# An attention-times-value kernel: v loaded for eight heads at a time, out stored for eight heads at a time

## Chip, cores, metric

One core of a Trainium2 chip. Times are device microseconds of one execution. Before the change: median 1056.14 us of 3 runs (1055.9 to 1057.2).

## The reference

```python
batch, n_heads, seq, head_dim = 8, 12, 1024, 64
# attn_weights: (8, 12, 1024, 1024) float32 = 403 MB;  v and out: (8, 12, 1024, 64) float32 = 25 MB each
out = np.einsum('bhqs,bhsd->bhqd', attn_weights, v)
```

## The kernel before

96 heads are worked as 24 groups of four (`q`), each group as two units (`n`). 128 partitions hold four heads x 32. A unit is one load of attn of 8.4 MB, cast to bf16 on its way into one of two buffers `abf`. TensorE transposes it (line 124), DVE and ACT copy the transposes out of PSUM, TensorE multiplies with v (line 166), transposes the product back (line 151), and ACT copies the rows into a slot of `osb`. In the first unit of a group v is spread over partitions by TensorE (line 139). GpSimd issues nearly all DMAs; SyncE counts their landings and passes them on. The parts that matter here:

```python
def pe_unit(i, n, loaded, it):                      # TensorE
    pe.wait_ge(*loaded)
    for g in range(G):
        ...
        transpose_g(abf[i], g, n)
    if i == 0:
        pe.wait_ge(s_vr, it)
        spread_v(range(VH), po + px)
        wait_both(s_vbf, it * 2)
    transpose_back()
    ...                                             # multiply
with nc.Fori(1, NV + 1, 1, engines=(PE,)) as it:    # 24 turns, two units each
    ...

def load_v(iv):                                     # GpSimd, 1 MB read
    pool.dma_start(out=vr.rearrange("p b x -> p (b x)"), in_=v_g[iv]).then_inc(s_v, 16)

def store(q, by_sync=False):                        # 1 MB written
    eng = nc.sync if by_sync else pool
    eng.wait_ge(s_out, 2 * q + 3)
    eng.dma_start(out=out_q[q], in_=osb[slot(q)].rearrange("p r d -> p (r d)"),
                  **({} if by_sync else {"single_packet": True}),
    ).then_inc(s_end if by_sync else s_osb[slot(q)], 16)

for n in range(NU - 2):
    pool.wait_ge(s_t[True], (n + 1) * PER_DVE)      # unit n is transposed, its buffer is free
    load_attn(n + 2)
    if n % 2 == 0:
        q = n // 2
        for s in s_sp:
            pool.wait_ge(s, 2 * q + 2)              # v of group q has been spread
        if q + 1 < NV:
            load_v(q + 1)
        if 0 < q <= HELD_FROM:                      # HELD_FROM = 17
            store(q - 1)
for q in range(HELD_FROM, BY_SYNC):                 # held until after the last load: 17, 18, 19
    store(q)
# SyncE: 20, 21, 22 and the pieces of 23, after the last load has landed
```

Of the kernel before, what the change touches and what calls it, by code (L numbers as in the profile page):

```python
# [10 lines left out]
def kernel(  # L11
# [18 lines left out]
    nc = tc.nc  # L30
    fp32 = mybir.dt.float32
    bf16 = mybir.dt.bfloat16
# [3 lines left out]
    D = v.shape[-1]  # L36
    NH = B * H
    P = 128
    VH = 4
    VP = P // VH  # L40
    G = Q // VP // 2
# [3 lines left out]
    SB = S // P  # L45
    VB = S // VP // SB
    NV = NH // VH
    NU = 2 * NV


    HELD = 6
    HELD_FROM = NV - 1 - HELD
    BY_SYNC = HELD_FROM + 3

    BY_EIGHTS = HELD_FROM // 2
    NO = 2 + NV - 2 * BY_EIGHTS

    HALVED = NU - 2

    def slot(q):  # L60
        return q % 2 if q < 2 * BY_EIGHTS else q - 2 * BY_EIGHTS + 2

    attn_q = attn_weights.rearrange("b (hq four) (p r) s -> (b hq) (four p) (r s)", four=VH, p=VP)
    out_q = out.rearrange("b (hq four) (p r) d -> (b hq) (four p) (r d)", four=VH, p=VP)
    v_g = v.rearrange("b (hq four) (p r) d -> (b hq) (four p) (r d)", four=VH, p=VP)

    def on_dve(g):
        return g % 8 in (0, 2, 4, 5, 7)
# [1 line left out]
    def count_of(g):  # L70

        return sum(on_dve(x) == on_dve(g) for x in range(g + 1))
# [4 lines left out]
    with tc.tile_critical(no_gpsimd_drain=True):  # L77
        sem = tc.alloc_semaphore
        sb = lambda name, shape, dt: nc.alloc_sbuf_tensor(name, shape, dt).ap()
# [1 line left out]
        spread = sb("spread", [P, VB, P], bf16)  # L81
        abf = [sb(f"abf{i}", [P, G, S], bf16) for i in range(2)]
        at = sb("at", [P, G, KW, P, 2], bf16)
        v32 = sb("v32", [P, VB, SB * D], fp32)
        vr = sb("vr", [P, VB, SB * D], bf16)
        vbf = sb("vbf", [P, SB, VH, D], bf16)
        ot = sb("ot", [P, GH, P], fp32)
        osb = [sb(f"osb{i}", [P, 2 * G, D], fp32) for i in range(NO)]
        bank = [nc.alloc_psum_tensor(f"bank{i}", [P, 512], fp32).ap() for i in range(8)]
        pt = [b.rearrange("p (k j) -> p k j", k=KW) for b in bank[:4]]  # L90
        po = bank[4:6]
        px = bank[6:8]
# [2 lines left out]
        s_abf = [sem(f"s_abf{i}") for i in range(2)]  # L95
        s_second = {n: sem(f"s_second{n}") for n in range(HALVED, NU)}
        s_v0, s_v = sem("s_v0"), sem("s_v")
        s_osb = [sem(f"s_osb{i}") for i in range(NO)]
        s_end = sem("s_end")

        s_t = {True: sem("s_t_dve"), False: sem("s_t_act")}
        s_sp = [sem("s_sp_dve"), sem("s_sp_act")]
# [8 lines left out]
        s_out, s_fin = sem("s_out"), [sem("s_fin0"), sem("s_fin1")]  # L111
        s_memset, s_const, s_vr = sem("s_memset"), sem("s_const"), sem("s_vr")
# [4 lines left out]
        pe = nc.tensor  # L117
# [13 lines left out]
                )  # L131
            last.then_inc(s_t[on_dve(g)])

        def spread_v(heads, banks):

            for h, ps in zip(heads, banks):
                rows = ds(h * VP, VP)
                for b in range(VB):
                    last = pe.matmul(  # L139
                        out=ps,  # L140
                        lhsT=spread[rows, b],
                        rhs=vr[rows, b],
                        start=(b == 0),
                        stop=(b == VB - 1),
                    )
                last.then_inc(s_sp[h % 2])
# [29 lines left out]
        def wait_both(s, n):  # L176
            for x in s:
                pe.wait_ge(x, n)

        def pe_unit(i, n, loaded, it):  # L180

            pe.wait_ge(*loaded)
            for g in range(G):
                if g == GH:
                    pe.wait_ge(s_half, n)
                transpose_g(abf[i], g, n)
            wait_both(s_ot, n)
            if i == 0:
                pe.wait_ge(s_vr, it)
                spread_v(range(VH), po + px)  # L190
                wait_both(s_vbf, it * 2)
            transpose_back()
            wait_both(s_last, n)
            for hp in range(2):
                for h in range(2):
                    for half in range(2):
                        outs = po[hp][ds(half * D, D), ds(h * GH * VP, GH * VP)]
                        last = multiply(outs, 2 * hp + h, half)
                last.then_inc(s_m[hp])
# [12 lines left out]
        def engine(dve):  # L212
            eng = nc.vector if dve else nc.scalar
# [4 lines left out]
            def spread_copy(h, ps, count):  # L218
                eng.wait_ge(s_sp[e], count)
                copy(  # L220
                    out=vbf[:, :, h], in_=ps.rearrange("p (k d) -> p k d", k=SB)
                ).then_inc(s_vbf[e])
# [7 lines left out]
                )  # L230

            def rows_of(n):
                return osb[slot(n // 2)][:, ds(n % 2 * G, G)]

            def back_copies(rows, count, free=None):
                if free is not None:
# [26 lines left out]
            def unit(n, base, rows, free):  # L263

                of_t, of_sp, of_back, of_m = base
                for g in mine:
                    copy_g(g, of_t + (n * per + count_of(g)))
                if n % 2 == 0:
                    spread_copy(e, po[e], of_sp + (n + 1))
                    spread_copy(2 + e, px[e], of_sp + (n + 2))  # L270
                if not dve:
                    back_copies(rows, of_back + 2 * n, free)
                product(of_m + (n + 1))


            un, iters = (2, NV) if dve else (4, BY_EIGHTS)
            with nc.Fori(1, iters + 1, 1, engines=(DVE if dve else ACT,)) as it:
                base = [eng.snap(it * (un * k) - un * k) for k in (per, 1, 2, 1)]
                of_free = None if dve else eng.snap(it * 2 - 2)
                for n in range(un):  # L280
                    rows = osb[(n - 1) // 2 % 2][:, ds((n - 1) % 2 * G, G)]
                    unit(n, base, rows, of_free + (n + 1) // 2 if n % 2 == 1 and not dve else None)
            for n in range(un * iters, NU):
                unit(n, (0, 0, 0, 0), rows_of(n - 1), None)
            k = 1 - e
            back_copy(rows_of(NU - 1), 4 * k, 4, px[k], 2 * NU + k + 1).then_inc(s_fin[k])

# [3 lines left out]
        for h in range(2):  # L291
            nc.vector.memset(ot[:, :, ds(h * HP, HP)], 0.0).then_inc(s_ot[h])
        nc.vector.wait_ge(s_v0, 16)
        nc.vector.tensor_copy(out=vr, in_=v32).then_inc(s_vr)  # L294
        engine(True)
        engine(False)


        pool = nc.gpsimd
# [8 lines left out]

        def load_v(iv):
            pool.dma_start(  # L310
                out=vr.rearrange("p b x -> p (b x)"), in_=v_g[iv]
            ).then_inc(s_v, 16)

        def store(q, by_sync=False):
            eng = nc.sync if by_sync else pool
            eng.wait_ge(s_out, 2 * q + 3)
            eng.dma_start(  # L317
                out=out_q[q],
                in_=osb[slot(q)].rearrange("p r d -> p (r d)"),
                **({} if by_sync else {"single_packet": True}),  # L320
            ).then_inc(s_end if by_sync else s_osb[slot(q)], 16)

        load_attn(0)
        load_attn(1)
# [2 lines left out]
            out=ident,  # L327
            in_=ident,
            compare_op=mybir.AluOpType.not_equal,
            fill=1.0,  # L330
            base=0,
# [4 lines left out]
        for h in range(VH):  # L336
            pool.wait_ge(s_const, h + 1)
            pool.affine_select(  # L338
                out=spread[ds(h * VP, VP)],
                in_=spread[ds(h * VP, VP)],  # L340
                compare_op=mybir.AluOpType.not_equal,
                fill=1.0,
                base=0,
                pattern=[[1, VB], [-1, P]],
                channel_multiplier=VB,
            ).then_inc(s_const)
        for n in range(NU - 2):
            pool.wait_ge(s_t[True], (n + 1) * PER_DVE)
            load_attn(n + 2)
            if n % 2 == 0:  # L350
                q = n // 2
                for s in s_sp:
                    pool.wait_ge(s, 2 * q + 2)
                if q + 1 < NV:
                    load_v(q + 1)
                if 0 < q <= HELD_FROM:
                    store(q - 1)
        for q in range(HELD_FROM, BY_SYNC):
            store(q)
        pool.drain()  # L360


        nc.sync.dma_start(out=v32.rearrange("p b x -> p (b x)"), in_=v_g[0]).then_inc(s_v0, 16)
        nc.sync.sem_inc(s_free, 2)
        for n in range(-2, NU - 2):

            if n + 2 < HALVED:
                nc.sync.wait_ge(s_abf[n % 2], 16 * ((n + 2) // 2 + 1))
            else:
                nc.sync.wait_ge(s_second[n + 2], 16)  # L370
            nc.sync.sem_inc(s_half)  # L371
            if n >= 0 and n % 2 == 0:
                q = n // 2
                nc.sync.wait_ge(s_v, 16 * (q + 1))
                nc.sync.sem_inc(s_vr)
                if 0 < q <= 2 * (BY_EIGHTS - 1):
                    nc.sync.wait_ge(s_osb[slot(q - 1)], 16 * ((q - 1) // 2 + 1))
                    nc.sync.sem_inc(s_free)
        for q in range(BY_SYNC, NV - 1):
            store(q, by_sync=True)  # L380
        rows = osb[slot(NV - 1)].rearrange("p (u half j) d -> p u half j d", u=2, half=2)
        outs = out_q[NV - 1].rearrange("p (u half j d) -> p u half j d", u=2, half=2, j=GH)
        nc.sync.wait_ge(s_out, NU)
        nc.sync.dma_start(out=outs[:, 0], in_=rows[:, 0]).then_inc(s_end, 16)
        for k in range(2):
            nc.sync.wait_ge(s_fin[k], 1)
            js = ds(4 * k, 4)
            nc.sync.dma_start(out=outs[:, 1, :, js], in_=rows[:, 1, :, js]).then_inc(s_end, 16)
        for q in range(2 * BY_EIGHTS - 2, BY_SYNC):
            nc.sync.wait_ge(s_osb[slot(q)], 16 * BY_EIGHTS if q < 2 * BY_EIGHTS else 16)  # L390
        nc.sync.wait_ge(s_end, 16 * (NV - 1 - BY_SYNC + 3))


# [28 lines left out]
```

## Time and profile before

| | before |
|---|---|
| DMA engines | full in every slice; GpSimd's queue 99.4% of the span |
| bytes at HBM | 453 MB, 430 GB/s |
| TensorE / DVE / ACT busy | 72% / 37% / 38% |
| DMAs | 50 loads of attn, 24 of v, 20 + 6 stores |

The first row bounds the kernel; the others have room. The prediction below shows the lines. From the DMA issues (tile, queue, count, KB at the destination, median us from issue to landing):

```profile
out_dram<-osb POOLq DMA_DIRECT2D x20, 1024.0 KB, 34.2
vr<-in_v_dram POOLq DMA_DIRECT2D x23, 512.0 KB, 34.3
```

The long time to landing is waiting in a full queue.

### The profile page before, as it was taken

What the parts mean: (1) busy time and instruction counts of PE and PEld (TensorE: products, weight loads), DVE (VectorE), ACT (ScalarE), POOL (GpSimd) and SP (SyncE); (2) the same over time, 40 slices, a digit from 0 to 9 for tenths busy, and PEclk for the clock granted to TensorE, in tenths of its full rate; (3) what the DMA queues carried; (4) which work ended last, traced back from release to release, by engine and by line L of the source; (5) the groups of instructions that cost most, each with busy time, mean ns of one, the idle gap of its engine ahead of it and who ended that gap; (6) DMA issues with size and microseconds to landing.
All of it is one profiled execution on the core that took longest, in us unless ns stands there. A gap on an engine that the chain in (4) does not pass through costs nothing.

```text
span 1053.3 us, 16277 instructions
## 1 busy us (share of the span) xinstructions
PE 754.8 (72%) x6920; PEld 709.4 (67%) x6920; DVE 387.9 (37%) x582; ACT 403.3 (38%) x489; POOL 52.4 (5%) x102
## 2 busy tenths in 40 slices
PE   0877686766867578775687766876678768777795
PEld 0776576766867568675686666866667668776785
DVE  1443343333443234432343333433335234433452
ACT  0443344433543334442353333433334334433452
POOL 1000000000000000000000000000000000000000
PEclk9989888888888888898888888888789898898898
DMA  9999999999999999999999999999999999999998
GB/s 219 220 217 208 234 236 218 238 209 247 233 218 238 207 243 239 217 238 209 244 236 215 234 219 237 238 219 234 227 228 234 215 218 218 218 218 215 210 217 322
DMA packets 14662, 239.67 MB, mean 228 GB/s; under 512 B 1600, under 2 KB 2112, under 8 KB 5184
## 3 DMA queue, kind: packets, MB, share of 16 engines
q0 software_dynamic: 13392, 234.36, 99.4%
q1 hardware_dynamic: 1264, 5.24, 1.3%
q8 instruction: 2, 0.03, 0.0%
q14 instruction: 4, 0.03, 0.0%
HBM read 427.82 MB, written 25.17 MB: 430 GB/s over the span
## 4 chain that ended last, share of the span: by engine, by line
DMA 76%; PE 23%; issue 1%; POOL 0%; DVE 0%; ACT 0%; SPq 0%; POOLq 0%
DMA abf<-in_attn_weights_dram 76%; PE bank L124 22%; PE bank L166 0%; PE bank L151 0%; POOL abf L304 0%; DVE osb L227 0%; ACT ot L256 0%; POOLq L417 0%; SPq L371 0%; SPq L77 0%
## 5 line engine op out<-in xcount | busy, mean ns | idle before, releaser
L124 PE MATMUL bank<-ident,abf 128*128 128x128 f32 x3072 | 470.8, 327 | 260.0 <-DMA abf<-in_attn_weights_dram 254.2
L124 PEld LDWEIGHTS bank<-ident,abf 128*128 128x128 f32 x3072 | 461.5, 215 | 272.8 <-DMA abf<-in_attn_weights_dram 266.7
L244 DVE COPY at<-bank 128x1024 bf16<-128x1024 bf16 x480 | 320.3, 689 | 495.1 <-PE bank L124 492.5
L244 ACT COPY at<-bank 128x1024 bf16<-128x1024 bf16 x288 | 289.2, 1012 | 428.1 <-PE bank L124 428.1
L166 PE MATMUL bank<-at,vbf 128*64 128x256 bf16 x3072 | 215.0, 278 | 0.0
L166 PEld LDWEIGHTS bank<-at,vbf 128*64 128x64 bf16 x3072 | 196.7, 108 | 13.4 <-DVE at L244 4.0
L256 ACT COPY ot<-bank 128x512 f32<-128x512 f32 x48 | 28.1, 586 | 181.1 <-PE bank L166 181.1
L256 DVE COPY ot<-bank 128x512 f32<-128x512 f32 x48 | 33.2, 692 | 151.4 <-PE bank L166 151.4
L151 PE MATMUL bank<-ident,ot 128*128 128x128 f32 x392 | 52.2, 276 | 33.0 <-DVE vbf L220 32.2
L151 PEld LDWEIGHTS bank<-ident,ot 128*128 128x128 f32 x392 | 43.4, 141 | 45.0 <-DVE vbf L220 44.0
L304 POOL DMA_DIRECT2D abf<-in_attn_weights_dram x50 | 26.6, 532 | 896.4 <-PE bank L124 895.3
L227 ACT COPY osb<-bank 128x512 f32<-128x512 f32 x97 | 52.2, 589 | 22.5 <-PE bank L151 22.5
L220 DVE CAST vbf<-bank 128x512 bf16<-128x512 f32 x48 | 30.9, 686 | 6.6 <-PE bank L139 6.6
L220 ACT CAST vbf<-bank 128x512 bf16<-128x512 f32 x48 | 25.8, 589 | 11.8 <-PE bank L139 11.8
L139 PE MATMUL bank<-vr,spread 32*128 32x512 bf16 x384 | 25.7, 377 | 0.0
L139 PEld LDWEIGHTS bank<-vr,spread 32*128 32x128 bf16 x384 | 9.9, 92 | 6.9
L310 POOL DMA_DIRECT2D vr<-in_v_dram x23 | 12.1, 528 | 19.2 <-PE bank L139 18.8
L317 POOL DMA_DIRECT2D out_dram<-osb x20 | 10.7, 537 | 37.3 <-ACT osb L227 37.3
L244 ACT ACT_TABLE_LOAD x8 | 10.3, 1283 | 1.2 <-SPq L77 1.1
L294 DVE CAST vr<-v 128x2048 bf16<-128x2048 f32 x1 | 1.4, 1406 | 3.3 <-DMA v<-in_v_dram 3.3
L338 POOL TENSOR_SCALAR_AFFINE_SELECT spread<-spread 32x512 bf16<-32x512 bf16 x4 | 2.5, 629 | 0.6
L227 DVE COPY osb<-bank 128x512 f32<-128x512 f32 x1 | 0.7, 692 | 3.1 <-PE bank L151 3.1
(8 smaller groups left out, 2.1 us busy)
## 6 DMA issues: line engine op xcount, KB each, us to landing
abf<-in_attn_weights_dram POOLq DMA_DIRECT2D x46, 4096.0 KB, 33.2
out_dram<-osb POOLq DMA_DIRECT2D x20, 1024.0 KB, 34.2
vr<-in_v_dram POOLq DMA_DIRECT2D x23, 512.0 KB, 34.3
abf<-in_attn_weights_dram POOLq DMA_DIRECT2D x4, 2048.0 KB, 26.0
out_dram<-osb SPq DMA_DIRECT2D x3, 1024.0 KB, 11.8
v<-in_v_dram SPq DMA_DIRECT2D x1, 1024.0 KB, 4.9
out_dram<-osb SPq DMA_DIRECT2D x1, 512.0 KB, 7.8
out_dram<-osb SPq DMA_DIRECT2D x2, 256.0 KB, 3.0
```

The source lines that it names most:

```text
L124: last = pe.matmul(out=pt[g % 4][:, k], lhsT=words[:, k], rhs=ident, is_transpose=True, start=(k == 0), stop=(k == KW - 1),)
L139: last = pe.matmul(out=ps, lhsT=spread[rows, b], rhs=vr[rows, b], start=(b == 0), stop=(b == VB - 1),)
L151: last = pe.matmul(out=ps[:, ds(j * P, P)], lhsT=ot[:, j0 + j], rhs=ident, is_transpose=True, start=(j == 0), stop=(j == jn - 1),)
L166: last = pe.matmul(out=outs, lhsT=vbf[:, 2 * kw + par, h], rhs=at[:, ds(half * GH, GH), kw, ds(h * VP, VP), par], start=(n == 0), stop=(n ...
L220: copy(out=vbf[:, :, h], in_=ps.rearrange("p (k d) -> p k d", k=SB)).then_inc(s_vbf[e])
L227: return copy(out=rows.rearrange("p (half j) d -> p j half d", half=2)[:, ds(j0, jn)], in_=ps[:, ds(0, jn * P)].rearrange("p (j half d) -> ...
L244: ins = copy(out=at[:, g].rearrange("c k j two -> c (k j two)"), in_=bank[g % 4].bitcast(bf16),)
L256: copy(out=ot.rearrange("c j (h p) -> c h j p", h=VH)[:, ds(2 * e, 2)], in_=po[e].rearrange("c (h j p) -> c h j p", h=2, j=GH),).then_inc( ...
L304: pool.dma_start(out=abf[n % 2][:, ds(g0, gn)].rearrange("p g s -> p (g s)"), in_=attn_q[n // 2][:, ds((n % 2 * G + g0) * S, gn * S)],).th ...
L310: pool.dma_start(out=vr.rearrange("p b x -> p (b x)"), in_=v_g[iv]).then_inc(s_v, 16)
L317: eng.dma_start(out=out_q[q], in_=osb[slot(q)].rearrange("p r d -> p (r d)"), **({} if by_sync else {"single_packet": True}),).then_inc(s_ ...
L338: pool.affine_select(out=spread[ds(h * VP, VP)], in_=spread[ds(h * VP, VP)], compare_op=mybir.AluOpType.not_equal, fill=1.0, base=0, patte ...
```

## The change

The intent: fewer and larger DMAs for v and out. One DMA of v brings eight heads, so TensorE has to pick the half of `vr` by a branch; one store takes eight heads, so ACT's loop runs over sixteen heads (four slots of `osb`) to know its slots. Core of the diff (index helpers, the matching waits of SyncE and the shared buffer for the first v are cut):

```diff
-    HELD_FROM = NV - 1 - HELD          # 17
-    BY_SYNC = HELD_FROM + 3            # 20
+    HELD_FROM = NV - 8                 # 16
+    BY_SYNC = NV - 4                   # 20
...
-        vr = sb("vr", [P, VB, SB * D], bf16)
+        vr = sb("vr", [P, 2, VB, SB * D], bf16)
-        osb = [sb(f"osb{i}", [P, 2 * G, D], fp32) for i in range(NO)]
+        osb = sb("osb", [P, NO, 2 * G, D], fp32)
...
-                spread_v(range(VH), po + px)
+                odd = pe.snap((it - 1) % 2)
+                with pe.If(odd > 0):
+                    spread_v(1, po + px)
+                with pe.Else():
+                    spread_v(0, po + px)
...
-            un, iters = (2, NV) if dve else (4, BY_EIGHTS)
+            un, iters = (2, NV) if dve else (8, LOOPED // 4)
...
-                out=vr.rearrange("p b x -> p (b x)"), in_=v_g[iv]
+                out=vr.rearrange("p two b x -> p two (b x)"), in_=v_2[iv]
...
         for n in range(NU - 2):
+            q, i = n // 2, n % 2
+            if i == 0 and q % 2 == 1 and q + 1 < NV:
+                for s in s_sp:
+                    pool.wait_ge(s, 2 * q + 2)
+                load_v((q + 1) // 2)
             pool.wait_ge(s_t[True], (n + 1) * PER_DVE)
             load_attn(n + 2)
-            if n % 2 == 0:
-                q = n // 2
-                for s in s_sp:
-                    pool.wait_ge(s, 2 * q + 2)
-                if q + 1 < NV:
-                    load_v(q + 1)
-                if 0 < q <= HELD_FROM:
-                    store(q - 1)
+            if i == 0 and q % 2 == 0 and 0 < q <= HELD_FROM:
+                store_2(q - 2)
...
-        nc.sync.dma_start(out=v32.rearrange("p b x -> p (b x)"), in_=v_g[0]).then_inc(s_v0, 16)
+        nc.sync.dma_start(
+            out=v32.rearrange("p (two x) -> p two x", two=2), in_=v_2[0]
+        ).then_inc(s_v0, 16)
```

More of the change, by code (lines that the diff above doesn't have):

```diff
@@ L48 @@
     NU = 2 * NV
-    HELD = 6
-    HELD_FROM = NV - 1 - HELD
-    BY_SYNC = HELD_FROM + 3
-    BY_EIGHTS = HELD_FROM // 2
-    NO = 2 + NV - 2 * BY_EIGHTS
+    HELD_FROM = NV - 8
+    BY_SYNC = NV - 4
+    LOOPED = HELD_FROM
+    NO = 8 + 2
     HALVED = NU - 2
     def slot(q):
-        return q % 2 if q < 2 * BY_EIGHTS else q - 2 * BY_EIGHTS + 2
+        return q % 4 if q < LOOPED + 2 else q - LOOPED + 2
     attn_q = attn_weights.rearrange("b (hq four) (p r) s -> (b hq) (four p) (r s)", four=VH, p=VP)
     out_q = out.rearrange("b (hq four) (p r) d -> (b hq) (four p) (r d)", four=VH, p=VP)
-    v_g = v.rearrange("b (hq four) (p r) d -> (b hq) (four p) (r d)", four=VH, p=VP)
+    out_2 = out.rearrange("b h q d -> (b h) q d").rearrange(
+        "(hq two four) (p r) d -> hq (four p) two (r d)", two=2, four=VH, p=VP
+    )
+    v_2 = v.rearrange("b h q d -> (b h) q d").rearrange(
+        "(hq two four) (p r) d -> hq (four p) two (r d)", two=2, four=VH, p=VP
+    )
     def on_dve(g):
@@ L83 @@
         at = sb("at", [P, G, KW, P, 2], bf16)
-        v32 = sb("v32", [P, VB, SB * D], fp32)
-        vr = sb("vr", [P, VB, SB * D], bf16)
+        vr = sb("vr", [P, 2, VB, SB * D], bf16)
         vbf = sb("vbf", [P, SB, VH, D], bf16)
         ot = sb("ot", [P, GH, P], fp32)
-        osb = [sb(f"osb{i}", [P, 2 * G, D], fp32) for i in range(NO)]
+        osb = sb("osb", [P, NO, 2 * G, D], fp32)
+        v32 = osb[:, ds(NO - 2, 2)].rearrange("p n r d -> p (n r d)")
         bank = [nc.alloc_psum_tensor(f"bank{i}", [P, 512], fp32).ap() for i in range(8)]
@@ L97 @@
         s_v0, s_v = sem("s_v0"), sem("s_v")
-        s_osb = [sem(f"s_osb{i}") for i in range(NO)]
-        s_end = sem("s_end")
+        s_osb = [sem(f"s_osb{i}") for i in range(2)]
+        s_held, s_end = sem("s_held"), sem("s_end")
         s_t = {True: sem("s_t_dve"), False: sem("s_t_act")}
@@ L132, in transpose_g, with spread_v @@
             last.then_inc(s_t[on_dve(g)])
-        def spread_v(heads, banks):
-            for h, ps in zip(heads, banks):
+        def spread_v(two, banks):
+            for h, ps in enumerate(banks):
                 rows = ds(h * VP, VP)
@@ L141, in spread_v @@
                         lhsT=spread[rows, b],
-                        rhs=vr[rows, b],
+                        rhs=vr[rows, two, b],
                         start=(b == 0),
@@ L232, in rows_of @@
             def rows_of(n):
-                return osb[slot(n // 2)][:, ds(n % 2 * G, G)]
+                return osb[:, slot(n // 2), ds(n % 2 * G, G)]
             def back_copies(rows, count, free=None):
@@ L273, in unit @@
                 product(of_m + (n + 1))
-            un, iters = (2, NV) if dve else (4, BY_EIGHTS)
+            un, iters = (2, NV) if dve else (8, LOOPED // 4)
             with nc.Fori(1, iters + 1, 1, engines=(DVE if dve else ACT,)) as it:
                 base = [eng.snap(it * (un * k) - un * k) for k in (per, 1, 2, 1)]
-                of_free = None if dve else eng.snap(it * 2 - 2)
+                of_free = None if dve else eng.snap(it * 2 - 1)
                 for n in range(un):
-                    rows = osb[(n - 1) // 2 % 2][:, ds((n - 1) % 2 * G, G)]
-                    unit(n, base, rows, of_free + (n + 1) // 2 if n % 2 == 1 and not dve else None)
+                    rows = osb[:, (n - 1) // 2 % 4, ds((n - 1) % 2 * G, G)]
+                    free = of_free + n // 4 if n in (1, 5) and not dve else None
+                    unit(n, base, rows, free)
             for n in range(un * iters, NU):
-                unit(n, (0, 0, 0, 0), rows_of(n - 1), None)
+                free = LOOPED // 2 + 1 if n == un * iters + 1 else None
+                unit(n, (0, 0, 0, 0), rows_of(n - 1), free)
             k = 1 - e
@@ L293 @@
         nc.vector.wait_ge(s_v0, 16)
-        nc.vector.tensor_copy(out=vr, in_=v32).then_inc(s_vr)
+        nc.vector.tensor_copy(out=vr.rearrange("p two b x -> p (two b x)"), in_=v32).then_inc(s_vr, 2)
         engine(True)
@@ L310, in load_v, with store, store_2 @@
             pool.dma_start(
-                out=vr.rearrange("p b x -> p (b x)"), in_=v_g[iv]
+                out=vr.rearrange("p two b x -> p two (b x)"), in_=v_2[iv]
             ).then_inc(s_v, 16)
-        def store(q, by_sync=False):
-            eng = nc.sync if by_sync else pool
-            eng.wait_ge(s_out, 2 * q + 3)
+        def store(q, fours, eng, done):
+            eng.wait_ge(s_out, 2 * (q + fours) + 1)
+            at_slot = osb[:, ds(slot(q), fours)].rearrange("p n r d -> p n (r d)")
             eng.dma_start(
-                out=out_q[q],
-                in_=osb[slot(q)].rearrange("p r d -> p (r d)"),
-                **({} if by_sync else {"single_packet": True}),
-            ).then_inc(s_end if by_sync else s_osb[slot(q)], 16)
+                out=out_2[q // 2] if fours == 2 else out_q[q],
+                in_=at_slot if fours == 2 else at_slot[:, 0],
+                **({"single_packet": True} if eng is pool else {}),
+            ).then_inc(done, 16)
+        def store_2(q):
+            store(q, 2, pool, s_osb[q // 2 % 2] if q < HELD_FROM else s_held)
         load_attn(0)
@@ L347 @@
         for n in range(NU - 2):
+            q, i = n // 2, n % 2
[3 more added lines that the diff above has]
+                load_v((q + 1) // 2)
             pool.wait_ge(s_t[True], (n + 1) * PER_DVE)
             load_attn(n + 2)
-            if n % 2 == 0:
-                q = n // 2
-                for s in s_sp:
-                    pool.wait_ge(s, 2 * q + 2)
-                if q + 1 < NV:
-                    load_v(q + 1)
-                if 0 < q <= HELD_FROM:
-                    store(q - 1)
-        for q in range(HELD_FROM, BY_SYNC):
-            store(q)
+            if i == 0 and q % 2 == 0 and 0 < q <= HELD_FROM:
+                store_2(q - 2)
+        for q in range(HELD_FROM, BY_SYNC, 2):
+            store_2(q)
         pool.drain()
-        nc.sync.dma_start(out=v32.rearrange("p b x -> p (b x)"), in_=v_g[0]).then_inc(s_v0, 16)
+        nc.sync.dma_start(
+            out=v32.rearrange("p (two x) -> p two x", two=2), in_=v_2[0]
+        ).then_inc(s_v0, 16)
         nc.sync.sem_inc(s_free, 2)
@@ L373 @@
                 q = n // 2
-                nc.sync.wait_ge(s_v, 16 * (q + 1))
-                nc.sync.sem_inc(s_vr)
-                if 0 < q <= 2 * (BY_EIGHTS - 1):
-                    nc.sync.wait_ge(s_osb[slot(q - 1)], 16 * ((q - 1) // 2 + 1))
+                if q % 2 == 1 and q + 1 < NV:
+                    nc.sync.wait_ge(s_v, 16 * ((q + 1) // 2))
+                    nc.sync.sem_inc(s_vr, 2)
+                if q % 2 == 1 and 1 < q <= HELD_FROM:
+                    nc.sync.wait_ge(s_osb[(q - 3) // 2 % 2], 16 * ((q - 3) // 4 + 1))
                     nc.sync.sem_inc(s_free)
-        for q in range(BY_SYNC, NV - 1):
-            store(q, by_sync=True)
-        rows = osb[slot(NV - 1)].rearrange("p (u half j) d -> p u half j d", u=2, half=2)
+        store(NV - 4, 2, nc.sync, s_end)
+        store(NV - 2, 1, nc.sync, s_end)
+        rows = osb[:, slot(NV - 1)].rearrange("p (u half j) d -> p u half j d", u=2, half=2)
         outs = out_q[NV - 1].rearrange("p (u half j d) -> p u half j d", u=2, half=2, j=GH)
@@ L388 @@
             nc.sync.dma_start(out=outs[:, 1, :, js], in_=rows[:, 1, :, js]).then_inc(s_end, 16)
-        for q in range(2 * BY_EIGHTS - 2, BY_SYNC):
-            nc.sync.wait_ge(s_osb[slot(q)], 16 * BY_EIGHTS if q < 2 * BY_EIGHTS else 16)
-        nc.sync.wait_ge(s_end, 16 * (NV - 1 - BY_SYNC + 3))
+        for k in range(2):
+            nc.sync.wait_ge(s_osb[k], 16 * (HELD_FROM // 4))
+        nc.sync.wait_ge(s_held, 16 * (BY_SYNC - HELD_FROM) // 2)
+        nc.sync.wait_ge(s_end, 16 * 5)
 _INS = ['attn_weights', 'v']
```

## The prediction

> **What bounds the kernel now.** I read the page first (engine shares, slices, queues), then the chain that ended last in order of time, then the busy time by stretch, then the DMA issues and the end of the run.
>
> ```profile
> PE 754.8 (72%) x6920; PEld 709.4 (67%) x6920; DVE 387.9 (37%) x582; ACT 403.3 (38%) x489; POOL 52.4 (5%) x102
> DMA  9999999999999999999999999999999999999998
> q0 software_dynamic: 13392, 234.36, 99.4%
> HBM read 427.82 MB, written 25.17 MB: 430 GB/s over the span
> ```
>
> No compute engine is full, and the 16 DMA engines are full in every slice: the queue fed by GpSimd alone keeps them busy for 99.4% of the span. The GB/s row of the page shows only some 220 because the loads of attn and v are cast on the way and counted at their bf16 size; the bytes at HBM, 427.82 + 25.17 = 453 MB, are what moves, at 430 GB/s.
>
> The chain of waits names TensorE's transposes for 22%, but I do not take that as a bound. In order of time it reads:
>
> ```profile
> 480.20 9.18 PE bank L124 x64
> 489.38 0.28 issue
> 489.67 34.04 DMA abf<-in_attn_weights_dram
> 523.71 0.04 issue
> 523.75 9.54 PE bank L124 x64
> 533.29 0.28 issue
> 533.58 33.69 DMA abf<-in_attn_weights_dram
> ```
>
> The load issued at 533.58 lands 33.7 us later, but a load needs only about 19.3 us of transfer (below). The rest is standing in the queue behind an earlier load. So the transposes decide when a load is issued, not when it starts. The busy time in single units shows the same:
>
> ```profile
> 523.75:543.07 19.32, 14.81 (x136) 14.26 (x136) 7.32 (x11) 8.88 (x10) 0.53 (x1) 0.85 0.96 205
> 543.07:567.31 24.24, 16.49 (x153) 15.16 (x153) 8.66 (x13) 8.76 (x11) 1.59 (x3) 0.85 1.05 247
> ```
>
> The stretches run from one landed load to the next (the starts of TensorE's transposes at line 124); the columns are length, then PE, PEld, DVE, ACT, POOL busy, granted clock, DMA share, GB/s. The first stretch is one load of attn; the second is one load, one v and one store in the same queue. The length follows the bytes queued, not the engines' work.
>
> **Price of a DMA.** I took the landing of each DMA on the slowest of the 16 engines from the packet records of the trace (the last of its sixteen 4-byte completion packets). In steady state the distance between landings repeats to the nanosecond: a 4096 KB load (8.389 MB read) 19.323 us, a v load (1.049 MB read) 2.458 us, a store (1.049 MB) 2.451 us; sum of two loads, one v, one store 43.56 us, which is the stretch above. The last two units are loaded in halves: 9.686 us each, so 2 x 9.686 - 19.323 = 0.049 us is the price of one more DMA at equal bytes. Check: (19.323 - 0.049) us for 8.389 MB is 435.2 GB/s; 1.049 MB at that rate is 2.409 us, plus 0.049 gives 2.458 us, the v load as measured. So time in this queue = 0.049 us per DMA + bytes at 435.2 GB/s.
>
> **What the Trainium skill says.** "DMA: Bandwidth & Descriptors", section "Anatomy of one DMA — SWDGE (gpsimd) path", fits about 2.0 us fixed per DMA plus bytes at 436 GB/s, and puts most of the 2 us in completion latency. Taken as queue time that would make this change worth tens of us; the trace shows only 0.049 us of it between back-to-back DMAs, because the next one's data flows while the last completes. "Where 436 GB/s comes from" in the same page derives a ceiling of 435.2 GB/s; my 435.2 agrees, although that section expects about 358 at HBM to bind, which this trace does not show. "Issuing engines are not separate DMA queues" there says that DMAs from any engine share the same 16 DMA engines; so moving v's first load or a store between SyncE and GpSimd moves no bandwidth. "Advanced Engine Details and Errata", "Control Flow Timing", gives a branch 51 ns and a compare-and-branch 108 ns; the trace before has no if to check it by.
>
> **The change part by part.**
> - *v by eight heads.* 24 DMAs become 12 of twice the bytes (1 + 23 become 1 + 11, the first from SyncE). The contiguous run stays one partition's 8 KB per head group. Saved on the DMA engines: 12 x 0.049 = 0.59 us.
> - *out by eight heads.* GpSimd's 20 stores become 10 (8 in the loop, 2 held), SyncE's first 3 become 2: 11 fewer, 0.54 us. Bytes and 8 KB runs are unchanged.
> - *Order.* v now goes ahead of the next load on odd groups of four heads, after a wait for TensorE's spreading of v. In the waits GpSimd stood 18.8 us in 22 times for that, 0.86 us each, plus 0.53 us to issue. So one load in four is issued 1.4 us later. Margin: from a landed load to the issue of the next is 9.8 to 10.3 us and the load ahead of it needs at least 19.3, so the queue holds 9 us of work or more; where the 1.4 us falls a 2 MB store stands ahead as well and it holds about 12. No cost.
> - *TensorE's branch.* 24 times a remainder, a compare and a jump; an estimate of 0.3 us each from the skill's figures. TensorE waits for loads 254.2 us in 46 waits, 5.5 us each. The tightest unit will be one with spreading (17.9 us from first transpose to last multiply before) that now meets a 19.3 us gap: 1.4 us spare, and a late TensorE still has the 9 us above. No cost.
> - *ScalarE's loop of sixteen heads.* 8 units unrolled and 4 turns instead of 8. It loaded its table 8 times (10.3 us in all, 1.28 us each); about 4 now. ScalarE is 38% busy: no gain in time.
> - *Start.* SyncE's first v is 2 MB and not 1, so the first attn lands some 2.4 us later and TensorE starts later; that v is not loaded later, so the queue's total is the same.
> - *End.* Held stores grow by one group: 16 to 22 and the last, 8 MB, instead of 17 to 22 and the last, 7 MB. The last load then lands earlier, by the one store (2.45) and the overheads saved until then (about 0.95): 3.4 us, near 1030.9 instead of 1034.3. TensorE's last stretch keeps its length:
>
> ```profile
> 1034.35 6.25 PE bank L124 x32
> 1040.60 0.88 PE bank L151 x8
> 1041.47 4.42 PE bank L166 x64
> ...
> 1047.75 0.69 DVE osb L227
> ```
>
> From the last landing to the last copy is 14.1 us, then about 3.0 us for the last 256 KB store. Meanwhile 7 MB of stores need 7 x 2.43 = 17.0 us on the slowest engine: 1034.3 + 17.0 = 1051.3, and the DMA share falls to nothing at 1051 to 1052. Before, both paths end together. After, the stores need 8 x 2.43 = 19.4 plus about 0.3 for the last small rows: 1030.9 + 19.7 = 1050.6, while the chain has its last store issued 3.4 us earlier, near 1045. So the end will be the DMA queue alone, 0.7 to 1.0 us earlier.
>
> Sum: 23 DMAs fewer x 0.049 = 1.1 us. 1056.14 - 1.1 = 1055.0 us. Nothing else lies on the path.
>
> **Rivals.**
> 1. *A DMA's 2 us fixed cost is paid in the queue.* 23 x 2.0 = 46 us saved, about 1010 us. Against it: a v load with its full cost takes 2.458 us where its bytes alone take 2.409.
> 2. *The longer DMAs disturb.* Sixteen 8 KB runs per engine in two places 1 MB apart may move less well, or a 2 MB store as one packet may hold an engine too long. Losing 5% on the 50 MB of v and out (116 us of transfer) would be 6 us: 1061. For it: nothing seen. Against it: run length, bytes and engines are the same.
> 3. *TensorE becomes the bound through a slow branch.* It would have to cost over 5 us a turn to use up the spare in the average unit; 10 us a turn would give about +2 to +5 us per pair. Nothing in the profile suggests it.
> 4. *The end turns worse* because SyncE's 2 MB store and the last pieces stand behind one another: up to +2 us, 1057.
>
> **Range and chances.** The gain is a tenth of a per cent. The three runs before spread over 1.3 us (1055.9 to 1057.2), and one v load near 106 us took 1.5 us longer than all others for no reason I can see; such events can shift the result by as much as the change. So 1053.4 to 1056.8. Two per cent is 21 us: only rival 1 reaches that on the fast side, only something I have not seen on the slow side. Faster 0.01, same 0.97, slower 0.02.
>
> **What would show it right or wrong.** Right: DMA still in the nines throughout, the same 453 MB, q0 share over 99%; 11 v issues of 1024 KB, 10 stores of 2048 KB from GpSimd; lengths of 43.56 us on average per two units while stores run, down by under 0.1 us; load landings of 19.32 us without v or store and about 24.2 with either; last load landed about 3 us earlier; DMA full until 1050. Wrong: a DMA slice below nine in the middle, TensorE's waits for loads turning into waits of the loads for TensorE, v or store landings above 4.95 us per 2 MB, or an end of the span over 19.5 us + 3 after the last load.

## The result

1055.43 us median of 6 runs (1055.2 to 1055.63), against 1056.02 us (1055.51 to 1057.2) of the kernel before. The ratio is 0.9993, 95% interval 0.998 to 1.0006: no difference that the runs can secure. Ratios here are the mean time of one kernel's fast runs over that of the other's of the same rounds, so not quite the ratio of the medians.

The page of the changed kernel, the lines that answer to those shown of before (engines, DMA share, queue, bytes, issues):

```profile
PE 730.0 (69%) x6920; PEld 684.6 (65%) x6920; DVE 388.3 (37%) x582; ACT 397.6 (38%) x485; POOL 45.0 (4%) x80
DMA  9999999999999999999999999999999999999998
q0 software_dynamic: 12912, 233.84, 99.0%
HBM read 427.82 MB, written 25.17 MB: 430 GB/s over the span
out_dram<-osb POOLq DMA_DIRECT2D x10, 2048.0 KB, 29.5
vr<-in_v_dram POOLq DMA_DIRECT2D x11, 1024.0 KB, 17.4
```

Half the DMAs of v and out, the same bytes, the same full DMA engines. v now takes 17.4 us from issue to landing because it stands in front of a load instead of behind it (put behind it again in an experiment below, it takes 32.2). With the engines full in the middle, only the bytes, the price of each DMA, single delays of transfers, and the two ends of the run are left to make a difference.

How much they did shorten it can be seen in the starts of TensorE's transposes, which follow the landings. First the kernel before, then the changed one (in order of time, PE alone: start, us busy, instruction, count, idle before and its releaser):

```profile
523.75 9.53 PE L124 MATMUL bank<-ident,abf 128*128 128x128 f32 x64 [6.76 <-DMA abf<-in_attn_weights_dram]
...
610.86 10.19 PE L124 MATMUL bank<-ident,abf 128*128 128x128 f32 x64 [6.01 <-DMA abf<-in_attn_weights_dram]
```

```profile
524.03 9.87 PE L130 MATMUL bank<-ident,abf 128*128 128x128 f32 x64 [6.41 <-DMA abf<-in_attn_weights_dram]
...
611.11 10.55 PE L130 MATMUL bank<-ident,abf 128*128 128x128 f32 x64 [7.09 <-DMA abf<-in_attn_weights_dram]
```

Eight heads, that is four loads, 2 MB of v and 2 MB of out, take 87.11 us before and 87.08 after. The packet records give it more finely, as landings on the slowest of the 16 DMA engines (the last of a DMA's sixteen completion packets, as in the prediction): 87.110 and 87.087 us, period after period. In single DMAs: a 2 MB v takes 4.896 us where two of 1 MB took 2 x 2.458 = 4.916; a 2 MB store 4.897 where two took 2 x 2.451 = 4.902. Taking a DMA away saved 0.020 us for v and 0.005 us for out, not 0.049.

The end of the span. In the changed kernel the last chain is (start, us, what):

```profile
1031.99 4.11 PE bank L130 x32
1036.10 0.87 PE bank L157 x8
1036.97 4.42 PE bank L172 x64
...
1043.25 0.69 DVE osb L237
```

It ends 4.5 us earlier than before (1043.25 and not 1047.75), of which 2.36 us is the earlier last load and 2.14 us a shorter first transpose run, at a higher granted clock (1.00 and not 0.50 to 0.64). Yet the span is 1053.8 us against 1053.3. (The two profiled executions took 1055.60 us after and 1055.47 before; the profiled one of before is faster than all six counted above, so this pair shows none of the 0.6 us between the medians.) The stretches show why the end did not move. First before, then after; the last two columns are DMA share and GB/s:

```profile
1048.00:1049.00 1.00, 0.00 (x0) 0.00 (x0) 0.44 (x1) 0.00 (x0) 0.00 (x0) 1.00 0.66 264
1049.00:1050.00 1.00, 0.00 (x0) 0.00 (x0) 0.00 (x0) 0.00 (x0) 0.00 (x0) 0.83 1.01 355
1050.00:1051.00 1.00, 0.00 (x0) 0.00 (x0) 0.00 (x0) 0.00 (x0) 0.00 (x0) 0.50 0.59 206
1051.00:1052.00 1.00, 0.00 (x0) 0.00 (x0) 0.00 (x0) 0.00 (x0) 0.00 (x0) 0.50 0.04 14
```

```profile
1048.00:1049.00 1.00, 0.00 (x0) 0.00 (x0) 0.00 (x0) 0.00 (x0) 0.00 (x0) 0.50 1.02 379
1049.00:1050.00 1.00, 0.00 (x0) 0.00 (x0) 0.00 (x0) 0.00 (x0) 0.00 (x0) 0.50 0.55 199
1050.00:1051.00 1.00, 0.00 (x0) 0.00 (x0) 0.00 (x0) 0.00 (x0) 0.00 (x0) 0.50 0.17 59
1051.00:1052.00 1.00, 0.00 (x0) 0.00 (x0) 0.00 (x0) 0.00 (x0) 0.00 (x0) 0.50 0.03 9
```

In both the last packet of a store ends near 1051 (1051.26 before, 1051.41 after, in the packet records). Before, the engines ran partly dry at 1048 to 1049 (0.66) and filled again for the two last stores, which were issued after the last copy: TensorE's chain and the queue end together. In the changed kernel those two stores stand in a full queue, which alone sets the end. Their median time from issue to landing, before and after:

```profile
out_dram<-osb SPq DMA_DIRECT2D x2, 256.0 KB, 3.0
```

```profile
out_dram<-osb SPq DMA_DIRECT2D x2, 256.0 KB, 7.0
```

In the changed kernel no compute engine works in the four lines above, and what is left at the end is a share of 0.17 and then 0.03, half of one engine of 16: one DMA engine lags behind its fellows. The packet records say by how much: at the last attn landing the slowest stood 2.6 us behind the fastest (2.1 before).

### The profile page after: what moved, and what is told of

The parts are those of the page before. It is cut to its first block, busy times and chain, and to the rows that moved or that the text cites. A ratio compares the mean times of both kernels' runs of the same rounds, so it can differ in the third digit from the quotient of the medians.

```text
span 1053.8 us, 16280 instructions
## 1 busy us (share of the span) xinstructions
PE 730.0 (69%) x6920; PEld 684.6 (65%) x6920; DVE 388.3 (37%) x582; ACT 397.6 (38%) x485; POOL 45.0 (4%) x80
## 4 chain that ended last, share of the span: by engine, by line
DMA 78%; PE 20%; issue 1%; POOL 0%; DVE 0%; ACT 0%; SPq 0%; POOLq 0%
DMA abf<-in_attn_weights_dram 78%; PE bank L130 20%; PE bank L172 0%; PE bank L157 0%; POOL abf L317 0%; DVE osb L237 0%; ACT ot L266 0%; POOLq L436 0%; SPq L388 0%; SPq L82 0%
## 5 line engine op out<-in xcount | busy, mean ns | idle before, releaser
L130 PE MATMUL bank<-ident,abf 128*128 128x128 f32 x3072 | 446.0, 315 | 280.4 <-DMA abf<-in_attn_weights_dram 276.5
L130 PEld LDWEIGHTS bank<-ident,abf 128*128 128x128 f32 x3072 | 436.5, 214 | 293.2 <-DMA abf<-in_attn_weights_dram 288.6
L323 POOL DMA_DIRECT2D vr<-in_v_dram x11 | 7.7, 703 | 239.8 <-PE bank L145 239.8
L307 DVE CAST vr<-osb 128x4096 bf16<-128x4096 f32 x1 | 2.3, 2294 | 25.3 <-DMA osb<-in_v_dram 25.3
L330 POOL DMA_DIRECT2D out_dram<-osb x10 | 7.1, 715 | 28.6 <-ACT osb L237 28.6
## 6 DMA issues: line engine op xcount, KB each, us to landing
vr<-in_v_dram POOLq DMA_DIRECT2D x11, 1024.0 KB, 17.4
```

What stands on the lines that cost most here:

```text
L130: last = pe.matmul(out=pt[g % 4][:, k], lhsT=words[:, k], rhs=ident, is_transpose=True, start=(k == 0), stop=(k == KW - 1),)
L323: pool.dma_start(out=vr.rearrange("p two b x -> p two (b x)"), in_=v_2[iv]).then_inc(s_v, 16)
L330: eng.dma_start(out=out_2[q // 2] if fours == 2 else out_q[q], in_=at_slot if fours == 2 else at_slot[:, 0], **({"single_packet": True} if ...
```

## The experiments

All are edits of the changed kernel; their diffs are shortened here to the lines that carry the idea. A run, below, is one contiguous stretch of DRAM that goes to or from one partition: a whole load of attn is 128 packets of 32 KB at the destination in the packet records, one for each partition, so 8 runs for each of the 16 engines. The theory they test came out of the comparison: the run is bound by DMA throughout; a DMA more costs 0.005 to 0.020 us; most of the 0.049 us of the prediction was the price of eight further contiguous runs per engine; and single delays of loads in front of stores, up to 0.8 us each, are as large as the whole gain. The rival A/B split is in the first four expectations. "Against before" is the difference of the medians in the same rounds; the changed kernel has -0.59 us, and -0.55 us when run again.

### Merging alone taken back

```diff
+            for two in range(2):
-            pool.dma_start(out=vr..., in_=v_2[iv]).then_inc(s_v, 16)
+                pool.dma_start(out=vr[:, two]..., in_=v_2[iv][:, two]).then_inc(s_v, 16)
 # stores of two slots likewise, each slot its own DMA; waits count 32 and not 16
```

> The changed kernel with its merging alone taken back: each 2 MB transfer of v and of out is issued as two of 1 MB, one behind the other, at the same place in the queue; 21 DMAs more, runs of 8 KB as before. Theory A (a DMA more costs 0.005 to 0.020 us on the DMA engines; most of the 0.049 us I had read off the halved loads is the price of the eight further runs per engine): the pair of v takes 4.916 us in the landings and not 4.896, the pair of stores 4.902 and not 4.897, time 1055.7 (0.3 longer). Theory B (the prediction: 0.049 us a DMA): 4.945 for both pairs, time 1056.5 (1.1 longer). The times may not part them; the landings do.

Measured: 1055.83 us median (5 runs, 1055.6 to 1056.48), +0.26 against before, ratio 1.0003 (0.999 to 1.0016). The landings: v 2.458 twice, so 4.916 for the pair; eight heads take 87.113 us where nothing delays a load, against 87.087 merged and 87.110 before. Later in the run the slowest engine changes and the two landings of a pair are no longer read singly, but the period leaves 4.903 us for the pair of stores (A: 4.902, B: 4.945). So the merging is worth 0.026 us per eight heads, as A has it; B would have given 0.098. The time moved by about 0.8 us between the two kernels relative to before, which would suit B, but the intervals do not part 0.3 from 1.1, and the profiled executions differ by 0.23 us (1055.83 and 1055.60); the landings part them.

### The price of a run, alone

```diff
-        abf = [sb(f"abf{i}", [P, G, S], bf16) for i in range(2)]
+        abf = [sb(f"abf{i}", [P, GH, 2 * S + 32], bf16) for i in range(2)]
 # the transposes read the padded rows
...
-                    out=abf[n % 2][:, ds(g0, gn)].rearrange("p g s -> p (g s)"), in_=rows
+                    out=abf[n % 2][:, ds(g0 // 2, gn // 2), ds(0, 2 * S)],
+                    in_=rows.rearrange("p (e x) -> p e x", x=2 * S),
```

> The changed kernel with the same DMAs, but each attn load cut into eight runs of 8 KB per partition instead of one of 64 KB (the buffer in SBUF gets 64 bytes of padding behind every two rows, so that the runs cannot be joined). 56 runs more per engine and load. Theory A: 56 x 3.6 ns = 0.20 us a load, 19.52 us between landings, time about 1065 (+9.7). Theory B (price by the DMA alone): 19.323 us, time unchanged at 1055.4.

Measured: 1063.36 us median, +7.79 against before, ratio 1.0073 (1.0058 to 1.0087). In the landings a load takes 19.521 us, the 19.52 that A gave: 0.198 us for 56 runs, 3.5 ns each. The PE starts show it (same columns as above):

```profile
551.55 9.64 PE L130 MATMUL bank<-ident,abf 128*128 128x128 f32 x64 [9.23 <-DMA abf<-in_attn_weights_dram]
571.07 9.44 PE L130 MATMUL bank<-ident,abf 128*128 128x128 f32 x64 [2.03 <-DMA abf<-in_attn_weights_dram]
```

19.52 us between two loads with nothing between them. The count of DMAs is that of the changed kernel, so B, which priced DMAs alone, is refuted. The padding also moves where the rows begin in SBUF; that this is not what costs, the cut by rows below shows: without padding, (0.049 - 0.020) us for 8 runs more is 3.6 ns each. In time the run came 1.3 us short of A's +9.7 counted from the changed kernel (8.4): its loads have only 0.44 us of extra delays where the changed kernel's have 1.59.

### Loads cut by rows and by partitions

```diff
-            for g0, gn in pieces:                      # one DMA a load
+            cuts: rows (0, 8), (8, 8)                   # load_by_rows: twice the runs
+            cuts: partitions (0, 64), (64, 64)          # load_by_partitions: the same runs
```

> The changed kernel with each attn load cut in two DMAs by rows: 48 DMAs more and twice the runs (16 and not 8 per engine and load). Theories A and B alike: 19.372 us a load, time about 1057.8 (+2.35). It is the control for the cut by partitions: A says that the cut by rows costs 2 to 3 times the cut by partitions, B that they cost the same.

Measured: 1056.48 us, +0.91 against before, ratio 1.0009 (0.9996 to 1.0022). Each half 9.686 us, so 19.372 a load as both theories have it: 0.049 us = 0.020 for the DMA + 8 x 3.5 ns for its runs. The time rose 1.5 us and not 2.35 over the changed kernel; again the delays in front of stores were fewer, 0.4 us in all.

> The changed kernel with each attn load cut in two DMAs by partitions (0 to 63, 64 to 127): 48 DMAs more, the number of runs unchanged. Theory A: a load takes 19.34 us and not 19.323 between landings; time about 1056.4 (+1.0). Theory B: 19.372 us; time 1057.8 (+2.35). If half the partitions are reached worse by the 16 DMA engines, both are wrong and the load is much longer; then the run says nothing about A and B.

Measured: 1081.08 us (1076.63 to 1086.39), ratio 1.0248: the third case of the expectation. Even without v or store between them, loads stand 19.53 us apart in the PE starts at the least (580.87 to 600.40 us); in the packet records the halves take 9.67 to 10.11 us, median 9.90, and the times of the executions scatter over 10 us. Loading half the partitions at a time is slower for a reason that no run looked for, and the run says nothing on A and B.

### TensorE's branch

```diff
-                odd = pe.snap((it - 1) % 2)
-                with pe.If(odd > 0): ...
+                spread_v(two, po + px)      # loop unrolled over two groups, two is a constant
```

> The changed kernel without TensorE's branch: its loop is unrolled over eight heads, so that the half of v is known in each half of the body; all else unchanged. My theory (TensorE waits for loads every unit, the branch lies in that wait): same time within 0.3 us of 1055.4, TensorE's waits for loads about the same 276 us. Rival (the branch takes back part of the gain): about 0.8 us faster, as the prediction's 1.1 us less what was measured.

Measured: 1055.01 us, -0.78 against before, ratio 0.9993 (0.9979 to 1.0007), where the changed kernel has 0.9993. The branch costs nothing that can be seen. The intervals alone do not exclude the rival's 0.8 us; what speaks against it is that TensorE has time to spare before each unit. TensorE's waits for loads, first the changed kernel, then without the branch (engine, tile and line, releaser: us in total, times, longest):

```profile
PE bank L130 <- DMA abf<-in_attn_weights_dram: 276.5, 46, 28.1
```

```profile
PE bank L130 <- DMA abf<-in_attn_weights_dram: 269.6, 46, 27.8
```

TensorE waits some 6 us on average before a unit in both, and 1.1 us in the tightest that the timeline of the changed kernel shows in its middle (480 to 700 us).

### How late may TensorE be

```diff
                 odd = pe.snap((it - 1) % 2)
+                for _ in range(5):
+                    spread_v(0, po + px, count=False)
```

> The changed kernel with five idle repeats of the spreading of v in each group of four heads: 5 x 1.07 = 5.4 us more TensorE work in every second unit, 128 us in all; the result is unchanged. My theory (9 us of work always stand in the DMA queue, TensorE's lateness of up to about 4 us is made good in the next unit): same time within 0.5 us, except that nothing of it may fall in the last unit; TensorE's waits for loads fall from 276 us to about 150. Rival (TensorE is close enough to the path that its lateness issues loads late): up to 24 x 5.4 = 128 us longer, and at least the 4 us by which the tightest unit is late, in each of 12 pairs: 40 us.

Measured: 1057.64 us (1056.85 to 1058.72), +1.85 against before, ratio 1.0017 (1.0003 to 1.003), waits for loads down to 188 us. 128 us of added work cost 2.4 us over the changed kernel: far from the rival's 40 to 128, but not within the 0.5 us of mine. The landings show where: the first v came 1.9 us late (6.811 us and not 4.896), and near the end, where stores are held back, another v came 1.3 us late (6.189 us) and loads by 0.07 to 0.9 us. No load in front of a store was late in this profile. GpSimd, in order of time, about the first:

```profile
58.87 0.53 POOL L320 DMA_DIRECT2D abf<-in_attn_weights_dram  x1 [19.54 <-PE bank L130]
83.17 0.70 POOL L326 DMA_DIRECT2D vr<-in_v_dram  x1 [23.77 <-PE bank L145]
83.86 0.56 POOL L320 DMA_DIRECT2D abf<-in_attn_weights_dram  x1
```

The load ahead, issued at 58.87, is all that stands in the queue; it began when the one before it landed (TensorE starts on that at 67.67) and lasts 19.3 us. v is issued 15.5 us into it, its first packet moves at 84.90, and some of the engines run dry: in the packet records only 11 or 12 of the 16 are busy at 85.5 to 86.2. In the middle of the run a 2 MB store stands there as well. If that is right, the place of v in the order is at fault, and this should undo it:

```diff
+            pool.wait_ge(s_t[True], (n + 1) * PER_DVE)
+            load_attn(n + 2)
             if i == 0 and q % 2 == 1 and q + 1 < NV:
                 ...
                 load_v((q + 1) // 2)
-            pool.wait_ge(s_t[True], (n + 1) * PER_DVE)
-            load_attn(n + 2)
```

> The kernel with five idle repeats of the spreading of v (which took 1057.6), with v issued behind the next load of attn again, as in the kernel before, and not in front of it. In that run the first v landed 1.9 us late, since it and the load behind it waited for the longer TensorE unit and no store stood in the queue there; it had more such places at the end of the loop, where the stores are held. Theory: the loss comes from the new place of v in the order; with v behind the load all landings from the third to the last are 19.32 and 4.90 except in front of stores, time 1055.7. Rival (the late TensorE itself issues loads late, wherever v stands): again 1057 to 1058.

Measured: 1054.95 us, -0.75 against before, ratio 0.9991 (0.9977 to 1.0004), with the same 128 us of extra TensorE work; 0.75 us less than expected, and 0.2 less than the changed kernel in the same rounds. From the third landing on, all loads take 19.32 us and all 2 MB transfers 4.90, but for one load of 20.70 in front of the first store. The theory holds: TensorE's own lateness costs nothing that can be seen, v issued in front of the load makes it cost.

### Held stores moved back into the loop

```diff
-            if i == 0 and q % 2 == 0 and 0 < q <= HELD_FROM:
+            if i == 0 and q % 2 == 0 and 0 < q <= BY_SYNC:
                 store_2(q - 2)
-        for q in range(HELD_FROM, BY_SYNC, 2):
-            store_2(q)
```

> The changed kernel with the two held stores of GpSimd (heads groups 16 to 19, 4 MB) moved back into the loop, in front of the last loads: 4 MB instead of 8 MB is left after the last load. Bytes and DMAs unchanged. My theory (the end is the later of the stores' queue and TensorE's last unit, and the change moved the balance to the queue): the last load lands 9.8 us later, near 1041.7, then 11.9 us to the last copy and 3 us for the last store and 2 to the end: span about 1058.6 to 1060.8, 5 to 7 us longer. Rival (only the bytes count, wherever they stand): same time.

Measured: 1060.59 us (1059.55 to 1061.47), +4.80 against before, +5.4 over the changed kernel; ratio 1.0048 (1.0033 to 1.0064). The span of the profiled execution, 1057.7 us, lies 0.9 us below the expected range; the time is inside the expected 5 to 7 us. Same bytes and DMAs. The last load's second half starts its transposes at 1041.33. Stretches (columns as before):

```profile
1048.00:1050.00 2.00, 2.00 (x38) 1.95 (x34) 0.69 (x1) 0.00 (x0) 0.00 (x0) 1.00 0.95 391
1050.00:1052.00 2.00, 1.23 (x15) 0.97 (x11) 0.00 (x0) 0.58 (x1) 0.00 (x0) 1.00 0.52 207
1052.00:1054.00 2.00, 0.58 (x6) 0.34 (x4) 0.69 (x1) 0.58 (x1) 0.00 (x0) 1.00 0.15 49
```

With 4 MB left the DMA engines fall idle at 1050 to 1054 while TensorE finishes; with 8 MB, in the changed kernel, they stay full. Holding stores pays as long as it covers TensorE's last unit, and the change has enough.

### No stores in the loop

```diff
-            if i == 0 and q % 2 == 0 and 0 < q <= HELD_FROM:
-                store_2(q - 2)
-                    nc.sync.wait_ge(s_osb[(q - 3) // 2 % 2], 16 * ((q - 3) // 4 + 1))
```

> The changed kernel without the eight stores of its loop (16 of 24 groups of heads are not written: wrong on purpose, 16 MB less). In the changed kernel single loads took up to 0.8 us longer than 19.323 at the slowest engine (20.080, 19.825, 19.628), each the load in front of a store; 1.6 us in all. Theory (these delays come with the stores' writing): all loads at 19.323 or .324, time 8 x 4.897 + 1.6 = 40.8 us shorter, 1014.6. Rival (they come with something else): some loads still above 19.6, time 39.2 us shorter, 1016.2.

Measured: 1014.59 us (1014.5 to 1014.7; 16 of 24 groups are not written, as intended). From the third landing on every load takes 19.323 or 19.324 us. The time is the theory's 1014.6 and not the rival's 1016.2. So the delays come with the stores; by which mechanism no run shows, and stores alone are not enough: `more_tensor` has the same stores and no such delay. This also shows that each transfer still counts fully: 16 MB of stores less are 40.8 us less, 39.2 of them the transfers themselves by the sum of the expectation.

### The start as before

```diff
-        nc.sync.dma_start(out=v32..., in_=v_2[0])                 # 2 MB
+        nc.sync.dma_start(out=v32[:, ds(0, VB * SB * D)], in_=v_2[0][:, 0])   # 1 MB
         load_attn(0)
         load_attn(1)
+        pool.dma_start(out=vr[:, 1]..., in_=v_2[0][:, 1]).then_inc(s_v, 16)
```

> The changed kernel with its start as before: SyncE loads 1 MB of v for the first four heads, and the second 1 MB goes on GpSimd's queue behind the first two loads of attn, cast on the way. In the changed kernel the third landing of attn came at 65.97 us where the kernel before gives 63.10 + 2.41 = 65.51. Theory: 2 MB from SyncE beside the first loads cost those 0.15 to 0.46 us, and with 1 MB the landings are those of before: the third load of attn lands near 63.1, v's second half 2.46 later, and the time is 0.2 to 0.4 us below that of the changed kernel run beside it. Rival (the start is no worse, the engines only stand differently): landing behind v at 65.7 to 66.0 as in the changed kernel, same time.

> The changed kernel itself once more, to have it in the same rounds as the two below. 1055.4 within 0.3 us; 0.3 to 0.6 us below the kernel before of the same rounds.

Measured in the same rounds: 1055.23 us with the start split (-0.47 against before, ratio 0.9994), 1055.15 us for the changed kernel again (-0.55, ratio 0.9993). In the landings the theory half holds: three loads of attn and two MB of v are in at 65.34 us, against 65.78 in the changed kernel's second profile. (These two times and those of the expectation count from a point 1.4 to 1.5 us after the start of the span; counted from its start, as the other times here, they are 66.86 and 67.32.) So 2 MB from SyncE beside the first loads cost 0.4 to 0.5 us there, but the time is the same and not 0.2 to 0.4 us less as expected; in that profile the load before the first store was delayed by 1.35 us. What the start is worth in time stays open.

No version beats the changed kernel by more than the runs scatter, so none is proposed.

## Why the prediction was right, and where a size was off

- **The bound.** Right: the DMA engines are full from the first load to near the last store, at 430 GB/s before and after.
- **"So time in this queue = 0.049 us per DMA + bytes at 435.2 GB/s."** This is the term that was mis-sized. Halving a load had doubled not only the DMAs but the contiguous runs per engine, from 8 to 16; that the v load fitted the formula was no check, since it, too, has 8 runs. The eight-run experiment prices a run at 3.5 ns, the merged v a DMA at 0.020 us, the merged store at 0.005 us. The sum becomes 12 x 0.020 + 11 x 0.005 = 0.3 us in place of 1.1 us, and in the landings the start takes as much back (third attn landing 67.37 us after the start of the span against 64.59 + 2.41 = 67.00).
- **The time.** 0.6 us lies between the medians, and what it consists of stays open. The DMAs give 0.3 us, the start takes about 0.4 us back, and delays of loads in front of stores came to 1.59 and 1.38 us in two profiles of the changed kernel, where in the one of before a single v was late by 1.5 us. In the two profiled executions this cancels: 1055.47 us before, 1055.60 after. A small gain is likely all the same, though no interval secures it: in the last rounds all five runs of the changed kernel lie below all nine of before. The prediction's range allowed for such events, but it is 3.4 us wide and holds the time of before as well: that the result fell inside does not speak for the 1.1 us, and is so far luck.
- **Order of v.** No cost, right for this kernel: every v from GpSimd takes 4.895 or 4.896 us in the landings. But "where the 1.4 us falls a 2 MB store stands ahead as well" is not so at the first and the last two places; with a longer TensorE unit v there came late.
- **Branch and ACT's loop.** No cost that the runs can see, as predicted; ACT loaded its table 4 times (5.1 us) and not 8 (10.3).
- **The first v.** "The queue's total is the same" does not hold in the landings: there the larger first v costs the 0.4 us named above. What that is worth in time stays open.
- **The end.** "3.4 us, near 1030.9": the last load landed 2.36 us earlier, at 1031.99. The store that moved behind it gives 2.45 as predicted, but the DMAs saved until then 0.26 and not 0.95, and the start (0.4) and the delays (0.1 more than before) took that back. That the end becomes the DMA queue's alone was right, and so was the length of the stores: 19.7 us predicted, 19.8 from the last landing to the last packet (1031.65 to 1051.41). But "0.7 to 1.0 us earlier" was not: with the last load 1 us later than predicted, the stores stop near 1051 in both. "TensorE's last stretch keeps its length" was not right either (4.11 us and not 6.25 for its first transposes), nor "DMA full until 1050" (0.55 from 1049 on).
- **Rivals.** The 2 us of fixed cost is not paid in the queue: refuted by every landing. No disturbance by longer DMAs: 4.896 us for 2 MB, and delays of single transfers came before as well (1.50 us and 1.59). No worse end by 2 us: the last store packet ends 0.15 us later. TensorE not near the path: 128 us more of it cost 2.4 us, or nothing with v behind the load.

## What to carry to other kernels

When DMA engines are full, merging transfers that already follow one another saves only what lies between them: here 0.005 to 0.020 us a DMA. Look first at the bytes, then at the length of contiguous runs, which a merge leaves as it was. When you read a price off a difference, check what else differs: half a load was one DMA more and eight runs more. And an issue moved in front of another makes the second wait for everything the first waits for; that is free only while the queue holds more work than the wait.

## What the Trainium skill lacked or had wrong

- The Trainium skill's "DMA: Bandwidth & Descriptors", "Anatomy of one DMA — SWDGE (gpsimd) path": it fits a DMA at about 2.0 us + bytes and does not say what one DMA more costs in a full queue. Here 0.005 us (stores) to 0.020 us (v).
- The same page, "Why small descriptors are slow (HBM only)", has a fixed price of about 3 cycles per packet. An estimate from that and the 850 MHz of "Where 436 GB/s comes from" is 3 / 0.85 = 3.5 ns, and agrees: 3.5 ns per run and engine (56 runs more per engine made a load 19.521 us in place of 19.323). What the section lacks is only that the price is still there, though small, with runs of 8 KB.
- The same page, "Where 436 GB/s comes from", says that for HBM to SBUF the HBM side (about 358 GB/s) binds; here it does not: 430 GB/s over the whole span, 435.2 within a load. This program runs on one core, and elsewhere the page itself measures about as much (425 GB/s) for a core whose neighbour is idle; it is that one sentence that misleads.
- No page read says that stores among loads delay single loads: up to 0.76 us in the first profile of the changed kernel, 1.38 us at the most in another run, none without stores in the loop.
